# A hybrid decoder block: causal masks for two attention kinds move from TensorE matmuls to VectorE operands

## The chip, the cores and the metric

The kernel runs on one core of one Trainium2 chip. It is written in Python against the Bass and Tile libraries; a scheduler in Tile puts each engine's instructions into a fixed order when the program is built. The metric is the device time of one execution in microseconds (us), taken as the median of several runs.

Engines are named as the profile names them: PE is TensorE (PEld its weight loads), DVE is VectorE, ACT is ScalarE, POOL is GpSimd, SP is SyncE, which issues most DMAs.

## What is computed

One decoder layer on 1024 tokens of width 1024, with 16 meta tokens in front (1040 positions in all, T in the code). Three head groups work in parallel on the normalised input: stick-breaking attention (8 heads of 64), a Mamba-2 state-space mixer, and MLA (8 heads, keys of 64 + 32). Their outputs go through one output projection, and a SwiGLU feed-forward layer follows. The change touches the two attention kinds:

```python
def stick_breaking_attention(q, k, v, valid):
    ...
        mask = (kidx[None, :] < qidx[:, None]) & valid[None, :]
        z = jnp.einsum('bqhd,bkhd->bhqk', qb.astype(F32), kf) * scale
        log_1m = jnp.where(mask, jax.nn.log_sigmoid(-z), 0.0)
        between = lax.cumsum(log_1m, axis=3, reverse=True) - log_1m
        w = jnp.exp(jnp.where(mask, jax.nn.log_sigmoid(z) + between, -jnp.inf))
        return jnp.einsum('bhqk,bkhd->bqhd', w, vf)

def mla_attention(q, k, v, valid):
    ...
        mask = (kidx[None, :] <= qidx[:, None]) & valid[None, :]
        s = jnp.einsum('bqhd,bkhd->bhqk', qb.astype(F32), kf) * scale
        p = jax.nn.softmax(jnp.where(mask, s, -1e30), axis=-1)
        return jnp.einsum('bhqk,bkhd->bqhd', p, vf)
```

A query of stick-breaking attention sees the keys before itself; a query of MLA sees itself too. In a block of 128 queries only the last 128 keys need a mask; all earlier keys are visible.

## The kernel before

Numbers are kept to full precision by splitting each operand into a high part and a remainder (hi and lo, rounded fp32), so a product takes two or three matmuls. Attention is done per head in rows: a row is a block of 128 queries against all keys up to its end, 144 to 1040 columns, cut by `key_chunks` into one to three chunks of at most 512 columns, each in its own PSUM bank (`sc_ps`, a ring of three).

**Stick-breaking row** (`sb_row`, lines 688 to 705). For each chunk, from the last to the first, two matmuls give the scores (L696, L697). The chunk that ends the row gets a third one (L700): the identity times `sb_mask`, a 128 x 128 tile with -1e30 above the diagonal, which adds the mask to the last 128 columns. ScalarE then writes the sigmoid of -score/8 into the row tile `cm` (L702); a masked column becomes 1. When the row is complete, VectorE runs one scan from right to left over it (L704): `state = data0 * state + data1`, starting from 1, where data1 is a column of zeros, `zcol`, broadcast over the row. The result is the running product of the sigmoids. There are 8 heads of 8 rows, so 64 scans and 64 mask matmuls.

**MLA row** (`mla_row`, lines 983 to 1017). Three matmuls per chunk (L999 to L1001), and on the last chunk a fourth with `mla_mask` (L1004). VectorE takes the negated maximum of each chunk (L1006); if there is more than one chunk, a further small reduction takes the minimum over the chunks (L1011). That is the bias of ScalarE's exponential (L1014), which also sums each chunk; VectorE adds the sums (L1016). Again 64 rows: 24 of one chunk, 32 of two, 8 of three.

**Values.** `weighted_values` takes two rows (an odd and an even block): TensorE transposes them 128 columns at a time (L319 to L331) into the banks `ptm` and `ptg`, ScalarE and VectorE split these into hi and lo (L314, L315, L321, L322), and TensorE multiplies by the values into `pv` (L304 to L323).

**What fills the gaps.** Beside the stick-breaking rows the scheduler places dense projections (`dense_fm`, L147 to L149): the next head pair's keys and queries (L607 to L617 evacuate them), the step sizes of the state-space mixer (`step_sizes`, L428 to L461) and its convolution channels (L495 to L508). Beside MLA it places the gate units (L547 to L550). `step_sizes` transposes its result into a bank (`dtt`, L434), copies it on VectorE (`dx`, L441 to L443), and then needs exponentials on ScalarE (L445 to L447), for which ScalarE's function table is loaded and afterwards loaded back for the sigmoid.

The order on each engine comes from Tile's scheduler, which simulates a timeline from its own costs when the program is built; `high_priority` and `issue_after` push single groups. So an instruction that vanishes or changes its cost can move others on all engines.

[...]

## Time and profile before

| what | value |
|---|---|
| runs | 1745.85, 1749.13, 1754.57 us; median 1749.13 |
| profiled execution | span 1747.0 us, which is its own time here; no other is listed for it |
| mean granted TensorE clock | 0.993 of full speed |
| DMA | 222.35 MB, mean 127 GB/s |
| GpSimd busy | 719.9 us (41%) |
| stick-breaking rows | about 68 to 437 us |
| MLA rows | about 659 to 991 us |

The span runs from the first to the last instruction of one profiled execution. Busy times overlap between engines. A matmul's duration in a row reaches beyond the start of the next one, since matmuls are pipelined; how long one holds the engine is read from the distance between starts. "Releaser" is the instruction whose end let a waiting one start. In a line such as `L704 DVE TENSOR_TENSOR_SCAN cm<-cm,zcol 128x1040 ... x8 | 19.9, 2484 | 1.2` stand the source line, engine, operation, output and inputs, shape and count, then busy us in total, mean ns of one, and idle us of the engine before them.

### The profile page before, as it was taken

To read this page: it belongs to the slowest core of one execution; us is meant where nothing else is said; L and a number is where in the kernel's file an instruction comes from. 1 tells how busy PE (TensorE), PEld (TensorE's weight loads), DVE (VectorE), ACT (ScalarE), POOL (GpSimd) and SP (SyncE) were. 2 spreads that over 40 slices of the span, in tenths; PEclk is the share of its full clock that TensorE was granted. 3 is DMA by queue.
4 is the path that set the end of the run, shared out by engine and by line. 5 is a ranking of instruction groups with operands and counts; after the bars stand their busy time and mean duration, and the time that the engine had idled before them with its cause. 6 is when DMAs were issued, how large, how long until landed. Compare 5 with 4: busy or idle time off the path is not lost. (4 is left out here: it accounts for less than half of the span.)

```text
span 1747.0 us, 26605 instructions
## 1 busy us (share of the span) xinstructions
PE 1696.7 (97%) x9801; PEld 1490.7 (85%) x9801; DVE 1136.0 (65%) x1742; ACT 845.0 (48%) x1813; POOL 719.9 (41%) x514
## 2 busy tenths in 40 slices
PE   8989999999999999999999999999999999999998
PEld 7979989999987788998888888778888888878887
DVE  7777676778454654555575656975666665688644
ACT  7555565655477727666554425422222322343333
POOL 3233345344477647553321445635555455200012
PEclk9999999999999999999999999999999999999999
DMA  4222232122434556347321442123332223999602
GB/s 163 74 68 64 69 86 80 55 70 75 146 118 128 182 175 172 102 125 241 111 87 37 130 162 89 62 92 107 104 102 97 91 96 115 329 397 354 238 1 97
DMA packets 145639, 222.35 MB, mean 127 GB/s; under 512 B 24722, under 2 KB 84148, under 8 KB 145508
## 3 DMA queue, kind: packets, MB, share of 16 engines
q1 hardware_dynamic: 126112, 205.09, 36.0%
q10 hardware_dynamic: 19396, 15.56, 2.9%
q8 instruction: 77, 1.26, 0.3%
q14 instruction: 54, 0.44, 0.1%
HBM read 157.56 MB, written 63.04 MB: 126 GB/s over the span
## 5 line engine op out<-in xcount | busy, mean ns | idle before, releaser
L147 PE MATMUL d_ps<-hnh,whi 128*128 128x384 f32 (+6 forms) x744 | 249.6, 336 | 7.0 <-DVE KS L610 4.1
L148 PE MATMUL d_ps<-hnh,wlo 128*128 128x384 f32 (+6 forms) x744 | 245.5, 330 | 0.0
L149 PE MATMUL d_ps<-hnl,whi 128*128 128x384 f32 (+6 forms) x744 | 245.4, 330 | 0.0
L136 POOL TENSOR_TENSOR wlo<-wraw,whi 128x1024 fp32r<-128x1024 f32 (+1 forms) x57 | 137.1, 2405 | 231.0 <-ACT whi L134 224.4
L147 PEld LDWEIGHTS d_ps<-hnh,whi 128*128 128x128 f32 (+1 forms) x744 | 140.3, 189 | 11.9 <-issue 3.1
L148 PEld LDWEIGHTS d_ps<-hnh,wlo 128*128 128x128 f32 (+1 forms) x744 | 140.4, 189 | 2.8 <-issue 0.5
L149 PEld LDWEIGHTS d_ps<-hnl,whi 128*128 128x128 f32 (+1 forms) x744 | 140.1, 188 | 2.3
L1287 PE MATMUL b_ps<-T,wl 128*128 128x512 f32 x352 | 138.3, 393 | 1.3 <-POOL wl L1118 1.3
L1286 PE MATMUL b_ps<-T,wh 128*128 128x512 f32 x352 | 138.5, 394 | 0.8 <-ACT wh L1117 0.4
L1288 PE MATMUL b_ps<-T,wh 128*128 128x512 f32 x352 | 137.7, 393 | 1.3 <-DVE T L1118 1.3
L315 DVE TENSOR_TENSOR pl<-ptg,ph 128x512 fp32r<-128x512 f32 (+1 forms) x160 | 99.8, 627 | 41.7 <-ACT ph L314 40.5
L1117 ACT CAST op<-raw 128x1024 fp32r<-128x1024 f32 x69 | 71.3, 1050 | 111.0 <-PE d_ps L1572 73.5
L1118 DVE TENSOR_TENSOR op<-raw,op 128x1024 fp32r<-128x1024 f32 x69 | 84.2, 1230 | 43.4 <-ACT op L1117 43.4
L704 DVE TENSOR_TENSOR_SCAN cm<-cm,zcol 128x144 f32<-128x144 f32 (+3 forms) x64 | 103.5, 1622 | 8.7 <-ACT cm L702 8.4
L314 ACT CAST ph<-ptg 128x512 fp32r<-128x512 f32 (+1 forms) x160 | 85.9, 542 | 41.6 <-PE ptg L331 24.3
L1118 POOL TENSOR_TENSOR wlo<-raw,whi 128x1024 fp32r<-128x1024 f32 x18 | 46.2, 2568 | 110.0 <-ACT whi L1117 110.0
L134 ACT CAST whi<-wraw 128x1024 fp32r<-128x1024 f32 (+1 forms) x57 | 58.9, 1033 | 57.9 <-PE d_ps L149 32.3
L1118 POOL TENSOR_TENSOR wl<-raw,wh 128x512 fp32r<-128x512 f32 x46 | 75.1, 1639 | 27.3 <-ACT wh L1117 27.3
L1124 POOL TENSOR_TENSOR tt<-tt 128x512 f32<-128x512 f32 (+1 forms) x8 | 8.1, 1009 | 188.8 <-ACT tt L1642 188.7
L1117 ACT CAST wh<-raw 128x512 fp32r<-128x512 f32 x88 | 53.1, 616 | 66.1 <-PE b_ps L1288 66.0
L507 POOL TENSOR_TENSOR csig<-csig,cacc 128x384 f32<-128x384 f32 (+1 forms) x36 | 47.5, 1320 | 84.2 <-issue 40.7
L502 DVE SCALAR_TENSOR_TENSOR cacc<-d_ps,cw,cacc 128x384 f32<-128x384 f32 (+3 forms) x108 | 61.8, 572 | 29.4 <-ACT cacc L495 27.5
(442 smaller groups left out, 5176.1 us busy)
## 6 DMA issues: line engine op xcount, KB each, us to landing
raw<-in_w_down_dram SPq DMA_DIRECT2D x99, 256.0 KB, 5.4
s_hops<-gs SPq DMA_DIRECT2D x63, 256.0 KB, 2.0
raw<-s_hops SPq DMA_DIRECT2D x63, 256.0 KB, 5.4
raw<-in_w_gate_dram SPq DMA_DIRECT2D x22, 512.0 KB, 3.5
raw<-in_w_up_dram SPq DMA_DIRECT2D x22, 512.0 KB, 4.0
wraw<-in_w_o_dram SPq DMA_DIRECT2D x16, 512.0 KB, 3.6
wraw<-in_w_xbc_dram SPq DMA_DIRECT2D x12, 512.0 KB, 3.6
s_xs<-csig SPq DMA_DIRECT2D x24, 192.0 KB, 2.5
```

Of the source, the lines that this page charges most:

```text
L136: pool.tensor_tensor(lo[:, :cols], raw[:, :cols], f32(hi[:, :cols]), op=ALU.subtract)
L147: pe.matmul(ps[:m, :n], wh, mh, start=(kt == 0), stop=False)
L148: pe.matmul(ps[:m, :n], wl, mh, start=False, stop=False)
L149: pe.matmul(ps[:m, :n], wh, ml, start=False, stop=(kt == nkt - 1))
L314: act.copy(ph[:, :n], pt[:, :n])
L315: dve.tensor_tensor(pl[:, :n], pt[:, :n], f32(ph[:, :n]), op=ALU.subtract)
L704: dve.tensor_tensor_scan(rev, rev, zcol.to_broadcast([128, n_all]), 1.0, ALU.mult, ALU.add)
L1117: act.copy(hi, value)
L1118: eng.tensor_tensor(lo, value, f32(hi), op=ALU.subtract)
L1286: pe.matmul(banks[j], hi[:, ks], UH[u][k], start=start and k == 0, stop=False, skip_group_check=skip)
L1287: pe.matmul(banks[j], lo[:, ks], UH[u][k], start=False, stop=False, skip_group_check=skip)
L1288: pe.matmul(banks[j], hi[:, ks], UL[u][k], start=False, stop=stop and k == 3, skip_group_check=skip)
```

## The change

Both mask matmuls are removed. In a stick-breaking row the mask becomes the scan's second operand: `sb_mask` is now as wide as the longest row (1040 columns), zero except in the masked corner of its last 128 columns, where it is 1, and the scan computes `state = max(data0 * state, data1)`. The product never exceeds 1, so the maximum resets it to 1 at a masked column and changes nothing elsewhere. `zcol` goes.

In an MLA row the last chunk's reduction becomes `tensor_tensor_reduce`: it writes -(score + mask) back over the scores in PSUM and takes the minimum of that along the row. `mla_mask` is now 512 columns wide with -1e30 in its corner. With two chunks the reduction starts from the first chunk's result, so the small reduction over chunks remains only for rows of three. The exponential of the last chunk takes a scale of -1 to undo the negation.

The masks take some 5 KB more of each SBUF partition; the area reserved for DMA descriptors is set to 4096 bytes (last hunk).

```diff
-    sb_mask = const.tile([128, 128], F32R, name="sb_mask")
-    mla_mask = const.tile([128, 128], F32R, name="mla_mask")
-    for e, (m, base) in enumerate(((sb_mask, -1), (mla_mask, 0))):
-        full = scratch[:, 128 * (e + 1) : 128 * (e + 2)]
-        pool.memset(full, 0.0)
+    sb_mask = const.tile([128, T], F32, name="sb_mask")
+    mla_mask = const.tile([128, 512], F32, name="mla_mask")
+    for m, base, fill in ((sb_mask, -1, 1.0), (mla_mask, 0, NEG)):
+        pool.memset(m, 0.0)
+        last = m[:, m.shape[1] - 128 :]
         pool.affine_select(
-            out=full, in_=full, pattern=[[-1, 128]], compare_op=ALU.is_ge, fill=NEG,
+            out=last, in_=last, pattern=[[-1, 128]], compare_op=ALU.is_ge, fill=fill,
             base=base, channel_multiplier=1,
         )
-        act.copy(m, full)
...
-                last = c0 + n >= n_all
                 pe.matmul(ps[:, :n], qs, Kh[:, c0 : c0 + n], start=True, stop=False)
-                pe.matmul(ps[:, :n], qs, KSh[:, c0 : c0 + n], start=False, stop=not last)
-                if last:
-                    m0 = n_all - 128 - c0
-                    pe.matmul(ps[:, m0 : m0 + 128], identr, sb_mask, start=False, stop=True)
-                    n = n_all - c0
+                pe.matmul(ps[:, :n], qs, KSh[:, c0 : c0 + n], start=False, stop=True)
                 act.activation(cm[:, c0 : c0 + n], ps[:, :n], AF.Sigmoid, scale=-0.125)
             rev = cm[:, 0:n_all][:, ::-1]
-            dve.tensor_tensor_scan(rev, rev, zcol.to_broadcast([128, n_all]), 1.0, ALU.mult, ALU.add)
+            dve.tensor_tensor_scan(rev, rev, sb_mask[:, T - n_all :][:, ::-1], 1.0, ALU.mult, ALU.max)
...
-                last = c0 + n >= n_all
+                last = x == nch - 1
...
-                pe.matmul(ps[:, :n], qh, KL[:96, c0 : c0 + n], start=False, stop=not last)
+                pe.matmul(ps[:, :n], qh, KL[:96, c0 : c0 + n], start=False, stop=True)
                 if last:
-                    m0 = n_all - 128 - c0
-                    pe.matmul(ps[:, m0 : m0 + 128], identr, mla_mask, start=False, stop=True)
-                    n = n_all - c0
-                dve.tensor_reduce(sm[:, x : x + 1], ps[:, :n], AX.X, ALU.max, negate=True)
+                    dve.tensor_tensor_reduce(
+                        ps[:, :n], ps[:, :n], mla_mask[:, 512 - n :], -1.0, sm[:, 0:1] if nch == 2 else -NEG,
+                        ALU.add, ALU.min, sm[:, x : x + 1],
+                    )
+                else:
+                    dve.tensor_reduce(sm[:, x : x + 1], ps[:, :n], AX.X, ALU.max, negate=True)
                 banks.append((ps, c0, n))
-            bias = sm[:, 0:1]
-            if nch > 1:
+            bias = sm[:, nch - 1 : nch]
+            if nch > 2:
                 bias = sm[:, 3:4]
                 dve.tensor_reduce(bias, sm[:, 0:nch], AX.X, ALU.min)
             for x, (ps, c0, n) in enumerate(banks):
                 acc = total if nch == 1 else sm[:, 4 + x : 5 + x]
-                act.activation(pr[:, c0 : c0 + n], ps[:, :n], AF.Exp, bias=bias, accum_out=acc)
+                sign = -1.0 if x == nch - 1 else 1.0
+                act.activation(pr[:, c0 : c0 + n], ps[:, :n], AF.Exp, scale=sign, bias=bias, accum_out=acc)
...
-    nc = bacc.Bacc("TRN2", target_bir_lowering=False, num_devices=1)
+    nc = bacc.Bacc("TRN2", target_bir_lowering=False, num_devices=1, dynamic_dma_scratch_size=4096)
```

Line numbers of the changed kernel are 3 to 8 lower than before from the masks on. The instruction orders of the two programs differ at many places before the feed-forward part. Three of them are shown, each as the order of before and then of the change.

VectorE at the first rows of stick-breaking attention, head 0, where the copies of the step sizes stand. `cm` is a row of scores, `dx` the step sizes, `dtt` the bank that they come from, `pm` the split of the meta columns; SCALAR_TENSOR_TENSOR is how the order names the scan.

```order
L704 SCALAR_TENSOR_TENSOR cm<-cm,zcol 128x400
L441 MEMSET dx 128x16
L322 TENSOR_TENSOR pm<-ptm,pm 16x256
L704 SCALAR_TENSOR_TENSOR cm<-cm,zcol 128x528
L442 COPY dx<-dtt 16x16
L443 COPY dx<-dtt 128x128
```
```order
L696 SCALAR_TENSOR_TENSOR cm<-cm,sb_mask 128x400
L696 SCALAR_TENSOR_TENSOR cm<-cm,sb_mask 128x528
L438 MEMSET dx 128x16
L319 TENSOR_TENSOR pm<-ptm,pm 16x256
L439 COPY dx<-dtt 16x16
L440 COPY dx<-dtt 128x128
```

The scan over 528 columns stood between the meta columns' split and the copies of the step sizes; it now stands ahead of both.

TensorE at the same place, from the transposes of the meta columns (`ptm`) on. `K`, `KS` and `Q` are the split keys and queries, `d_ps<-hnh,whi` the dense projection of the next keys, which goes on behind the last row of each piece.

```order
L319 MATMUL ptm<-identr,cm 16x128
L320 MATMUL ptm<-identr,cm 16x128
L696 MATMUL sc_ps<-K,Q 128x256
L697 MATMUL sc_ps<-KS,Q 128x256
L700 MATMUL sc_ps<-sb_mask,identr 128x128
L696 MATMUL sc_ps<-K,Q 128x272
L697 MATMUL sc_ps<-KS,Q 128x272
```
```order
L316 MATMUL ptm<-identr,cm 16x128
L317 MATMUL ptm<-identr,cm 16x128
L692 MATMUL sc_ps<-K,Q 128x256
L693 MATMUL sc_ps<-KS,Q 128x256
L692 MATMUL sc_ps<-K,Q 128x400
L693 MATMUL sc_ps<-KS,Q 128x400
L692 MATMUL sc_ps<-K,Q 128x384
L693 MATMUL sc_ps<-KS,Q 128x384
```

Here the score tiles of 400 and 384 columns, which stood behind most of the dense projection, come before it; the 272-column tile that stood here has moved ahead of the transposes.

VectorE among the first rows of MLA, head 0. `sc_ps` is a chunk of scores, `sm` the small tile of a row's minima and sums, `inv` a row's total, `pl` the lower part of a split; ISA is how the order names the two instructions of `tensor_tensor_reduce`.

```order
L322 TENSOR_TENSOR pm<-ptm,pm 16x256
L1006 TENSOR_REDUCE sm<-sc_ps 128x1
L315 TENSOR_TENSOR pl<-ptg,ph 128x384
L1016 TENSOR_REDUCE inv<-sm 128x1
L1006 TENSOR_REDUCE sm<-sc_ps 128x1
L1011 TENSOR_REDUCE sm<-sm 128x1
```
```order
L319 TENSOR_TENSOR pm<-ptm,pm 16x256
L312 TENSOR_TENSOR pl<-ptg,ph 128x384
L1000 TENSOR_REDUCE sm<-sc_ps 128x1
L1011 TENSOR_REDUCE inv<-sm 128x1
L995 ISA sc_ps,sm<-sc_ps,mla_mask,sm 128x256
L995 ISA sm 128x1
```

The second chunk's reduction and the minimum over the two chunks have become the pair of L995: one instruction over the 256 columns and one of a single column behind it.

## Prediction

> **What bounds the kernel now.** I read the busy table first, then busy time by stretch, then what TensorE waited for, then single mask matmuls in the timeline.

> ```profile
> span 1747.0 us, 26605 instructions
> PE 1696.7 (97%) x9801; PEld 1490.7 (85%) x9801; DVE 1136.0 (65%) x1742; ACT 845.0 (48%) x1813; POOL 719.9 (41%) x514
> ```

> TensorE (PE) is busy for 97% of the span and VectorE (DVE) for 65%. A share over the whole run says little about two stages, so here are the stretches that hold the stick-breaking rows (68 to 437 us) and the MLA rows (660 to 991 us). Columns: stretch, its length, then busy time of PE, weight loads, DVE, ACT and POOL, then the granted clock.

> ```profile
> 68.00:180.00 112.00, 102.53 (x648) 95.48 (x647) 80.26 (x130) 58.98 (x129) 45.95 (x36) 0.97 0.26 74
> 180.00:310.00 130.00, 128.10 (x920) 123.39 (x920) 86.19 (x123) 77.09 (x182) 54.58 (x46) 1.00 0.27 76
> 310.00:437.00 127.00, 126.28 (x855) 122.42 (x855) 98.43 (x139) 73.83 (x168) 50.08 (x34) 1.00 0.21 67
> 660.00:770.00 110.00, 107.45 (x758) 104.84 (x757) 53.79 (x131) 77.22 (x200) 68.26 (x60) 1.00 0.45 129
> 770.00:880.00 110.00, 107.48 (x683) 96.92 (x682) 62.66 (x137) 63.15 (x164) 42.83 (x34) 1.00 0.52 162
> 880.00:991.00 111.00, 109.25 (x628) 94.26 (x628) 76.74 (x144) 56.55 (x134) 26.57 (x13) 1.00 0.28 84
> ```

> TensorE idles 9.5, 1.9, 0.7, 2.6, 2.5 and 1.8 us there: 19 us in 700, half of it in the first stretch. VectorE has 104 of 369 us free beside the stick-breaking rows and 138 of 331 beside MLA. The waits of TensorE (total, times, longest), the two largest of the stick-breaking stretch and the largest of MLA:

> ```profile
> PE d_ps L147 <- DVE KS L610: 4.1, 3, 1.8
> PE sc_ps L696 <- ACT cm L702: 3.9, 1, 3.9
> ...
> PE sc_ps L999 <- ACT pr L1014: 1.7, 2, 1.1
> ```

> No wait repeats row after row: transposes, values and dense projections of other heads fill TensorE while a row is scanned or exponentiated. What leaves TensorE there should leave the span, except just ahead of the few waits.

> **Removed: 128 mask matmuls.** The grouped rows give their count:

> ```profile
> L700 PE MATMUL sc_ps<-sb_mask,identr 128*128 128x128 f32 x64 | 15.2, 238 | 0.0
> L1004 PE MATMUL sc_ps<-mla_mask,identr 128*128 128x128 f32 x64 | 15.0, 235 | 0.0
> ```

> Their 235 ns is no price, since matmuls overlap; starts are. One MLA mask and one stick-breaking mask (start, duration), and the weight loads round the latter:

> ```profile
> 765.90 0.22 PE L1004 MATMUL sc_ps<-mla_mask,identr 128*128 128x128 f32 x1
> 765.96 0.34 PE L999 MATMUL sc_ps<-mhi 96*128 96x272 f32 x1
> 766.14 0.28 PE L1000 MATMUL sc_ps<-mhi,mlo 96*128 96x272 f32 x1
> 766.26 0.29 PE L1001 MATMUL sc_ps<-mlo,mhi 96*128 96x272 f32 x1
> ```
> ```profile
> 86.22 0.22 PE L700 MATMUL sc_ps<-sb_mask,identr 128*128 128x128 f32 x1
> 86.28 0.39 PE L147 MATMUL d_ps<-hnh,whi 128*128 128x384 f32 x1
> 86.51 0.34 PE L148 MATMUL d_ps<-hnh,wlo 128*128 128x384 f32 x1
> 86.68 0.34 PE L149 MATMUL d_ps<-hnl,whi 128*128 128x384 f32 x1
> ```
> ```profile
> 86.22 0.19 PEld L147 LDWEIGHTS d_ps<-hnh,whi 128*128 128x128 f32 x1
> 86.33 0.19 PEld L148 LDWEIGHTS d_ps<-hnh,wlo 128*128 128x128 f32 x1
> ```

> The next matmul starts 0.06 us after a mask, but the one behind it comes late. In MLA the 272-column matmul after the mask holds TensorE for 0.18 us (765.96 to 766.14), its equal for 0.12 (766.14 to 766.26). So mask and successor take 0.24 where the successor alone takes 0.12: the mask costs 0.12. In the other spot 0.29 less 0.17 gives 0.12 again. The reason is in the weight-load rows: loads follow each other by 0.11 us at the closest, and a 0.06 us matmul cannot cover one. I take 0.115 us: 128 x 0.115 = 14.7 us, 0.84% of the span. Bounds are 0.06 (7.7 us) and 0.12 (15.4 us).

> [...]

> Not all of it shortens the span: masks shortly ahead of a wait that another engine ends only lengthen that wait. Columns here: stretch, length, busy time (count) of these matmuls.

> ```profile
> 68.00:94.00 26.00, 1.38 (x6) 1.14 (x6) 0.99 0.43 108
> ```
> ```profile
> 658.00:676.00 18.00, 1.17 (x5) 0.95 (x5) 1.00 0.59 166
> ```

> Six masks lie ahead of the 3.9 us wait (ending at 93.5), five round the first MLA rows. I give back 11 x 0.115 = 1.3 us.

> **Added on VectorE, stick-breaking.** No instruction: the scan reads a 1040-wide mask where it read a broadcast column, and takes a maximum where it added. Its rows:

> ```profile
> L704 DVE TENSOR_TENSOR_SCAN cm<-cm,zcol 128x1040 f32<-128x1040 f32 x8 | 19.9, 2484 | 1.2 <-ACT cm L702 1.2
> L704 DVE TENSOR_TENSOR_SCAN cm<-cm,zcol 128x784 f32<-128x784 f32 x8 | 19.1, 2390 | 0.8 <-ACT cm L702 0.7
> L704 DVE TENSOR_TENSOR_SCAN cm<-cm,zcol 128x912 f32<-128x912 f32 x8 | 17.9, 2242 | 1.2 <-ACT cm L702 1.2
> ...
> L704 DVE TENSOR_TENSOR_SCAN cm<-cm,zcol 128x272 f32<-128x272 f32 x8 | 5.7, 716 | 0.0
> ```

> From 272 to 1040 columns it takes (2484 - 716) / 768 = 2.3 ns a column, twice the pace of the reductions below (1.0 ns). A pace so far under that of plain reading is more likely set by the running product than by the second operand, so I take no change. A third more or less is the bound; the price above is a rival below.

> **Added on VectorE, MLA.** Each of 64 rows trades a reduction of its last chunk for a fused instruction, and the order shows a second, 128x1 one behind each: "one instruction" is two. In the 32 rows of two chunks the minimum of two columns goes. Nearest rows:

> ```profile
> L1006 DVE TENSOR_REDUCE sm<-sc_ps 128x1 f32<-128x400 f32 x32 | 18.1, 565 | 5.3 <-PE sc_ps L1001 4.1 <-PE sc_ps L1004 0.8
> ...
> L1006 DVE TENSOR_REDUCE sm<-sc_ps 128x1 f32<-128x272 f32 x24 | 10.4, 434 | 3.5 <-PE sc_ps L1001 2.6 <-PE sc_ps L1004 0.7
> ...
> L1011 DVE TENSOR_REDUCE sm<-sm 128x1 f32<-128x2 f32 x32 | 4.7, 145 | 0.3
> ```
> ```profile
> L1014 ACT ACTIVATION_READ_ACCUMULATOR pr<-sc_ps,sm 128x1 f32 x112 | 22.4, 200 | 0.0
> ```

> The reduction's pace is (565 - 434) / 128 = 1.0 ns a column. The fused one makes a single pass too, so I take that pace; the far bound is the scan's 2.3. Over the last chunks' 8 x (144 + 272 + 400 + 256 + 256 + 384 + 512 + 384) = 20,864 columns that is 0 to 27 us. The second instruction lies between 0.145 us (a tiny reduction) and 0.200 (ScalarE's accumulator read): 64 of them are 9.3 to 12.8 us, less 32 x 0.145 = 4.6. VectorE gains 5 us, at the far end 35, against 138 free. In a two-chunk row the path from matmul to Exp keeps its length; in the other 32 it grows by 0.15 to 0.2 us, covered by other heads' matmuls. If a tenth of that cover fails, 1 us shows; I take 1, and 7 (a doubling of the MLA waits) as the far end.

> The rest has one answer. The sign in Exp's scale is free, and the smaller descriptor area touches nothing in the profile. The start loses two short ScalarE casts and gains wider memsets on GpSimd, which stands idle for 4.2 us ahead of its first product; that idle time hides them, and without it they would cost their own length of some 1 us.

> ```profile
> 7.80 1.28 POOL L231 TENSOR_TENSOR wk<-raw,wk 128x512 fp32r<-128x512 f32 x1 [4.16 <-ACT wk L230]
> ```

> **Moved: the order.** The scheduler laid out TensorE's order anew up to the first row sums of the feed-forward part; from there on it is unchanged.

> ```profile
> 1056.77 0.72 PE L158 MATMUL d_ps<-ones,sq 128*128 128x1 f32 x6
> ```

> At the 3.9 us wait two things move, both shown with the change: the 528-column scan now stands ahead of the step-size copies, and two score tiles are pulled forward. The rows of before:

> ```profile
> 84.84 2.73 DVE L704 TENSOR_TENSOR_SCAN cm<-cm,zcol 128x528 f32<-128x528 f32 x1
> 87.50 0.14 DVE L442 COPY dx<-dtt 16x16 f32<-16x16 f32 x1
> ```
> ```profile
> 93.54 0.70 PE L696 MATMUL sc_ps<-K,Q 128*128 128x400 f32 x1 [3.90 <-ACT cm L702]
> ...
> 95.23 0.52 PE L149 MATMUL d_ps<-hnl,whi 128*128 128x384 f32 x1
> 95.55 0.52 PE L147 MATMUL d_ps<-hnh,whi 128*128 128x384 f32 x1
> ```

> The copies end up to 2.7 us sooner, and ScalarE's table load and the sigmoid that frees the score bank hang on them. TensorE reaches its wait sooner too, having done the pulled-forward tiles. I take 1.0 us off; the bounds are 2.7 off and 1 on.

> **Sum.** -14.7 + 1.3 + 0 + 1.0 - 1.0 = -13.4 us, from 1747.0 to 1733.6. The profiled span lies 2.1 us under the median of the runs (1749.1), and I carry that over: **1736 us**, 0.77% faster. The nearest rows leave it between -7.7 + 1.3 + 7 + 1 (2 slower) and -15.4 - 2.7 (18 faster). An order that also loses a quarter of the 19 us of waits would reach 1727.

> **Rivals.** A measurement of this kernel can tell about 0.5% from no change: under 1740.4 is faster, over 1757.9 slower.

> *A mask costs only its own 0.06 us.* It frees 7.7 us, and after the other terms the run takes 1743: within 0.5%. For it speaks the step of 0.06 to the next start, against it the late matmul behind. [...]

> *The new order brings new stalls.* A stall like that of 93.5 costs more than its 3.9 us: afterwards 384-column matmuls start 0.32 us apart (95.23 to 95.55) against 0.17 before it (86.51 to 86.68). Nine to ten of them, up to 96.8, add 1.4 us. Two new stalls of 5.3 us give 1736 + 10.6 = 1747, no difference. For it speaks that the first stretch alone, with 9.5 us of idle, is reshuffled; against it that 180 to 437 us hold only 2.6 us of idle.

> *The scan pays for a true second operand.* If its 2.3 ns a column became half as much again, 8 x (144 + 272 + ... + 1040) = 37,888 columns would cost VectorE 43.6 us between 68 and 437. Its load there would go from 265 to 308 of some 362 us, and each row's transposes would wait up to 1.2 us longer. It decides from 22 us exposed, half of it: 60% gives 1736 + 26 = 1762, slower. Against it speaks the argument on the pace. For it speaks that something stretches scans already: 784 columns take longer in the mean than 912 (2390 and 2242 ns). [...]

> **Chances.** Forecast 0.68. The cheap mask 0.10 and new stalls 0.12, both within 0.5%. The scan, or anything of its size, 0.10, slower. The range of 1727 to 1750 takes in the first three cases and leaves out the last and the tails.

> **What would show it.** After: 9673 matmuls; masked chunks whose successor no longer holds 0.18 us; stick-breaking and MLA stretches shorter by about 7 us each with the same filler; scans at 2484 and 716 ns; fused instructions near 434 and 565 ns at 272 and 400 columns with 0.15 to 0.2 us behind. It is wrong if TensorE's idle time grows by over 5 us before 1057 us, if scans are over 10% longer, or if the stretch behind 1057 us changes.

## The result and the profile after

The changed kernel takes 1745.41 us (median of 20 runs, 1742.63 to 1750.33). The kernel before, on the same chip, takes 1750.86 (median of 20 runs). The ratio is 0.9969, 95% interval 0.9960 to 0.9978: 5.4 us faster, where 13.4 were forecast. The direction was right, and 1745.4 lies in the range, but 8.0 us of the forecast did not arrive.

The head of the page after:

```profile
span 1742.3 us, 26429 instructions
...
PE 1688.7 (97%) x9673; PEld 1479.6 (85%) x9673; DVE 1140.2 (65%) x1773; ACT 846.0 (49%) x1811; POOL 717.3 (41%) x514
```

There are 9673 matmuls, 128 fewer than before. VectorE has 4 us more work. The same six stretches as in the prediction (stretch, length, busy time of PE, weight loads, DVE, ACT and POOL, granted clock):

```profile
68.00:180.00 112.00, 100.68 (x609) 93.04 (x610) 79.06 (x127) 56.55 (x122) 39.56 (x34) 0.94 0.26 70
180.00:310.00 130.00, 127.69 (x915) 122.86 (x916) 89.82 (x128) 78.09 (x186) 53.94 (x45) 1.00 0.28 79
310.00:437.00 127.00, 127.00 (x858) 123.34 (x857) 95.69 (x141) 77.29 (x176) 51.00 (x37) 1.00 0.23 69
660.00:770.00 110.00, 107.42 (x758) 105.17 (x758) 58.30 (x154) 83.06 (x215) 71.49 (x63) 1.00 0.46 131
770.00:880.00 110.00, 107.04 (x664) 95.09 (x664) 65.50 (x152) 62.18 (x158) 35.95 (x29) 1.00 0.49 156
880.00:991.00 111.00, 109.86 (x619) 94.01 (x618) 74.01 (x149) 54.09 (x128) 38.40 (x16) 1.00 0.34 93
```

The five later stretches look as they did. The first one holds 609 matmuls, was 648, at a clock of 0.94, was 0.97, with 11.3 us idle, was 9.5. The waits of TensorE say where (total, times, longest):

```profile
PE sc_ps L692 <- ACT cm L694: 6.9, 2, 6.0
...
PE d_ps L144 <- DVE KS L607: 5.4, 3, 2.7
PE d_ps L1382 <- DVE hT L1091: 2.8, 1, 2.8
```

Of the 3.9 us wait ending at 93.5 us, 0.8 us is left (ending at 97.8), and a 6.0 us wait has come, almost at the start of the stick-breaking rows:

```profile
65.40 0.23 PE L692 MATMUL sc_ps<-K,Q 128*128 128x144 f32 x1
...
65.87 0.34 PE L692 MATMUL sc_ps<-K,Q 128*128 128x400 f32 x1
66.06 0.35 PE L693 MATMUL sc_ps<-KS,Q 128*128 128x400 f32 x1
72.44 0.58 PE L692 MATMUL sc_ps<-K,Q 128*128 128x256 f32 x1 [6.03 <-ACT cm L694]
72.82 0.42 PE L693 MATMUL sc_ps<-KS,Q 128*128 128x256 f32 x1
```

Three score tiles fill the three `sc_ps` banks, and nothing else can start. In before, the step-size projection stood there; its two possible banks (`d_ps`) are held by the third chunk's keys and queries until VectorE has subtracted them. VectorE at this place, before and then after:

```profile
62.88 0.55 DVE L617 TENSOR_TENSOR Q<-d_ps,Q 64x384 fp32r<-64x384 f32 x1
63.47 0.56 DVE L609 TENSOR_TENSOR K<-d_ps,K 64x384 fp32r<-64x384 f32 x1
64.04 0.56 DVE L610 TENSOR_TENSOR KS<-d_ps,K 64x384 fp32r<-64x384 f32 x1
64.63 5.31 DVE L276 TENSOR_TENSOR hnl<-xT,hnh 128x384 fp32r<-128x384 f32 x8
69.97 0.56 DVE L617 TENSOR_TENSOR Q<-d_ps,Q 64x384 fp32r<-64x384 f32 x1
```
```profile
64.53 0.55 DVE L614 TENSOR_TENSOR Q<-d_ps,Q 64x384 fp32r<-64x384 f32 x1
65.12 5.61 DVE L273 TENSOR_TENSOR hnl<-xT,hnh 128x384 fp32r<-128x384 f32 x8
70.75 0.56 DVE L606 TENSOR_TENSOR K<-d_ps,K 64x384 fp32r<-64x384 f32 x1
71.33 0.56 DVE L607 TENSOR_TENSOR KS<-d_ps,K 64x384 fp32r<-64x384 f32 x1
71.92 0.56 DVE L614 TENSOR_TENSOR Q<-d_ps,Q 64x384 fp32r<-64x384 f32 x1
```

Before, the second head's K and KS are done at 64.6 us, ahead of the eight `hnl` subtractions, so one bank is free, and projection and scores cover TensorE until the sigmoids start (it is busy for all of 60 to 76 us). After, they stand behind these eight, both banks are held until 71.9, and the sigmoids too wait for the last `hnl`. No mask matmul takes part in this: it is the order of the first phase.

### The profile page after: what moved, and what is told of

It is laid out like the page before. It is cut to its first block, busy times and chain, and to the rows that moved or that the text cites. A ratio compares the mean times of both kernels' runs of the same rounds, so it can differ in the third digit from the quotient of the medians.

```text
span 1742.3 us, 26429 instructions
## 1 busy us (share of the span) xinstructions
PE 1688.7 (97%) x9673; PEld 1479.6 (85%) x9673; DVE 1140.2 (65%) x1773; ACT 846.0 (49%) x1811; POOL 717.3 (41%) x514
## 4 chain that ended last, share of the span: by engine, by line
PE 80%; DVE 6%; DMA 6%; ACT 3%; issue 2%; POOL 2%; SPq 0%; ACTq 0%; DVEq 0%; POOLq 0%
PE d_ps L144 9%; PE d_ps L146 9%; PE d_ps L145 9%; PE b_ps L1283 8%; PE b_ps L1282 8%; PE b_ps L1281 8%; PE b_ps L1566 2%; PE b_ps L1567 2%; PE b_ps L1565 2%; PE ptg L326 2%; PE ptg L328 1%; PE pv L305 1%; PE pv L304 1%; DMA raw<-s_osbl 1%; PE sc_ps L991 1%
## 5 line engine op out<-in xcount | busy, mean ns | idle before, releaser
L696 DVE TENSOR_TENSOR_SCAN cm<-cm,sb_mask 128x144 f32<-128x144 f32 (+3 forms) x64 | 97.1, 1523 | 7.4 <-ACT cm L694 6.8
L1119 POOL TENSOR_TENSOR tt<-tt 128x512 f32<-128x512 f32 (+1 forms) x8 | 8.1, 1015 | 188.4 <-ACT tt L1637 188.2
L1282 PEld LDWEIGHTS b_ps<-T,wl 128*128 128x128 f32 x352 | 66.8, 190 | 17.4 <-POOL wl L1113 1.6
L1116 DVE TENSOR_TENSOR raw<-raw 128x512 f32<-128x512 f32 x58 | 53.2, 925 | 43.3 <-DMA raw<-in_w_gate_dram 38.4
```

The costliest lines, as they stand in the source:

```text
L696: dve.tensor_tensor_scan(rev, rev, sb_mask[:, T - n_all :][:, ::-1], 1.0, ALU.mult, ALU.max)
L1282: pe.matmul(banks[j], lo[:, ks], UH[u][k], start=False, stop=False, skip_group_check=skip)
```

## The experiments

**Theory A**: a removed mask is worth its 0.115 us, and stalls of the new order took most of the gain back. **Theory B**: a mask is worth its own 0.06 us (7.7 in all) and the order costs little. Later runs bear out A's price of a mask; where the gain went is only in part where A puts it. Each ratio is to the kernel before on the same chip.

**Last hunk alone** (`num_devices=1, dynamic_dma_scratch_size=4096`):

> The kernel before with the last hunk alone (descriptor area of 4096 bytes); every engine's order stays as it was. All theories: no change, within 1.5 us of the kernel before. It is run for what the 20 runs of before don't list: the granted clock of each run. Theory A (the removed masks were worth about 14.5 us, and new stalls with half-clock windows behind them took some 9 back): mean clock about 0.002 to 0.003 above the 0.990 of the changed kernel. Theory B (a mask was worth only 0.06 us, 7.7 in all, and the order cost little): mean clock like that of the changed kernel, 0.990.

Measured: 1.0010 (0.9999 to 1.0020), no change. The mean clock of 35 runs of before beside it is 0.9915, that of the changed kernel's 20 runs 0.9902, lower by half of what A expected. But the mean of the kernel before is 0.9907 and 0.9911 in the 11 and 17 runs beside later experiments on two other chips, so these means do not tell the two kernels apart. This run with the order of before also shows that a single trace misleads. TensorE loses 8.6 us to half clock in before's trace and 15.7 here (a granted clock of 0.50; 1 minus the clock, times busy time, summed over stretches of 2 us); the changed kernel's 14.0 is nothing special.

**Stick-breaking half alone** (the `sb_row` and `sb_mask` hunks; MLA as before):

> Stick-breaking half alone on the kernel before (mask as the scan's operand; MLA untouched). TensorE's order at the first stick-breaking rows is the one with five score tiles ahead of the step-size projection. Theory A: the 6 us wait near 66 us comes back, 64 x 0.115 = 7.4 us saved, about 3 us more idle time and 2.5 us more half clock given back up to 477 us: 2 us faster than before (0 to 4). Theory B: 64 x 0.06 = 3.8 us faster, with idle time and half clock as in before. Scans at 2484 and 716 ns at 1040 and 272 columns by both.

Measured: 1.0010 (0.9997 to 1.0022). Not 2 us faster but no change, so neither theory's number; the wait that A expected is there, 6.2 us.

**MLA half alone** (the `mla_row` and `mla_mask` hunks; stick-breaking rows as before):

> MLA half alone on the kernel before (stick-breaking rows with their mask matmuls; TensorE's first 3991 instructions stand as in before). Theory A: 64 x 0.115 = 7.4 us saved between 659 and 1057 us; the wait near 1012 us (2.8 us) and a half-clock window behind it come back and cost some 4: 3 us faster than before (1 to 5.5). Theory B: 3.8 us faster, and the stretch from 659 to 1057 us shorter by 3.8 apart from its idle time.

Measured: 0.9974 (0.9961 to 0.9987), 4.6 us faster by the ratio, with the 2.8 us wait for `hT`. By these two runs, the whole net gain of the change comes with the MLA half.

**Step-size projection put first.** In the changed kernel, the first four rows wait for that projection's matmuls:

```diff
+                        with ExitStack() as early:
+                            if p == 0 and h == 0 and i < 4:
+                                early.enter_context(tc.issue_after(dt_done[0 if i < 3 else 2]))
+                            rows.append(sb_row(Q[h], K[h], KS[h], i))
```

> The changed kernel with the step-size projection put ahead of the first score tiles; TensorE's order differs from the changed kernel in rows 369 to 551 only. Theory A (new stalls are what ate the gain): the 6.0 us wait at 66.4 us and its half-clock windows (2.5 us) go, some of the wait comes back at the later step-size chain: 4 to 8 us faster than the changed kernel, 1738 to 1741, about 0.6% under before. Theory B (masks were cheap, order counts little): within 1.5 us of the changed kernel's 1745.4.

Measured: 1.0009 (0.9995 to 1.0022): slower than the changed kernel, whose ratio is 0.9969. Both theories missed. The wait did not go; it changed its name:

```profile
65.26 0.28 PE L579 MATMUL v_ps<-wv,hnh 128*128 128x256 f32 x1
71.79 0.51 PE L144 MATMUL d_ps<-hnh,whi 128*96 128x272 f32 x1 [6.25 <-DVE KS L608]
```

Now the projection itself waits, for KS on VectorE. The first reading, "the scores stand in front of the projection", was wrong: the banks are what is missing, and VectorE's order keeps them. Beside it, a wait for KS has grown to 4.6 us (ending at 112.1; 2.7 in the changed kernel). In the traces the orders of before and of the changed kernel part on TensorE at 28.6 us, long ahead of any mask matmul, so something at the very start must have moved them. Laid side by side, the two programs differ there in nothing but the constants.

**One memset moved.** The kernel before with a single edit:

```diff
-    dve.memset(zcol, 0.0)
+    pool.memset(zcol, 0.0)
```

> The kernel before with one edit: the memset of the 128x1 column of zeros is issued on GpSimd instead of VectorE. All masks stay. By the scheduler's order this alone puts five score tiles ahead of the step-size projection, as in the changed kernel, and K, KS and Q of the third chunk behind eight hnl subtractions on VectorE; from TensorE's row 553 on its order is that of before. Theory A (the start's order, set by the constants, is what ate the stick-breaking half): a wait of about 6 us near 70 us, 3 to 8 us slower than before. Theory B (the order costs nothing, the stick-breaking masks were simply worth little): within 1.5 us of before.

Measured: 1.0036 (1.0022 to 1.0049), 6.3 us slower. Every mask is still on TensorE, and the new order with its wait is there all the same:

```profile
65.40 5.69 DVE L276 TENSOR_TENSOR hnl<-xT,hnh 128x384 fp32r<-128x384 f32 x8
71.12 0.56 DVE L609 TENSOR_TENSOR K<-d_ps,K 64x384 fp32r<-64x384 f32 x1
```
```profile
66.74 0.22 PE L700 MATMUL sc_ps<-sb_mask,identr 128*128 128x128 f32 x1
72.81 0.58 PE L696 MATMUL sc_ps<-K,Q 128*128 128x256 f32 x1 [5.85 <-ACT cm L702]
```

Up to the first mask matmul TensorE's order is that of the changed kernel. A 128x1 memset (0.06 us on VectorE in before's trace) is not worth 6 us of work, so the price is that of the order. The memset is one entry in the timeline that the scheduler simulates; how the simulation gets from there to this order is not shown. In the changed kernel other constants changed too; that the missing memset alone moves its start was not run.

**The changed kernel with the start of before.** The constants of before are still made, though no longer used, and the wide masks are built behind the first projections:

```diff
+    dve.memset(zcol, 0.0)
+    stand = const.tile([128, 256], F32R, name="stand")
+    ...  (two 128x128 masks filled and cast into stand, as before)
...
     p0_st.close()
+    for m, base, fill in ((sb_mask, -1, 1.0), (mla_mask, 0, NEG)):
+        ...
```

> The changed kernel with the start of before: the column of zeros and the two cast 128x128 masks are still made (and not used), the wide masks are built behind the first projections. TensorE's first 396 instructions are those of before. Theory A: no 6 us wait near 66 us; 6 us (the MLA half as measured) and 64 x 0.115 = 7.4 us less 1 us for masks ahead of the 3.9 us wait: 1735 to 1739, about 0.7% under before. Theory B: no faster than the MLA half alone, 1743, or only by 64 x 0.06 = 3.8 at most (1740 to 1743).

Measured: 0.9921 (0.9907 to 0.9935), median 1737.54: 13.8 us faster than before by the ratio, and faster than the changed kernel, whose interval starts at 0.9960. VectorE is back in the order of before, K and KS ahead of `hnl`:

```profile
63.91 0.56 DVE L610 TENSOR_TENSOR K<-d_ps,K 64x384 fp32r<-64x384 f32 x1
64.49 0.56 DVE L611 TENSOR_TENSOR KS<-d_ps,K 64x384 fp32r<-64x384 f32 x1
65.08 5.43 DVE L277 TENSOR_TENSOR hnl<-xT,hnh 128x384 fp32r<-128x384 f32 x8
```

The 6.0 us wait is gone, and before's wait of 3.9 us is back (3.7, ending at 93.2). That 13.8 comes close to the prediction's 13.4 is in part luck. The first MLA row and the first row sums of the feed-forward part, in the changed kernel and then in this run:

```profile
656.12 0.69 PE L991 MATMUL sc_ps<-mhi 96*128 96x144 f32 x3 [1.16 <-ACT mhi L971]
1049.35 0.72 PE L155 MATMUL d_ps<-ones,sq 128*128 128x1 f32 x6
```
```profile
658.88 1.14 PE L1003 MATMUL sc_ps<-mhi 96*128 96x144 f32 x3 [2.09 <-ACT mhi L983]
1051.09 0.72 PE L159 MATMUL d_ps<-ones,sq 128*128 128x1 f32 x6
```

Up to the row sums this run is hardly ahead of the changed kernel: 1051.1 us against 1049.4, or 1040.7 against 1041.9 with the loss to half clock taken off. TensorE's idle time up to there is 40.2 us against 40.7. The lead arises behind them, where no mask stood: 685.1 us to the end, against 692.9 in the changed kernel and 690.3 in before. The table below comes back to this.

**The same, and the `hT` wait at 1015 us taken away** (the two products of `rraw` with `grow` behind the last addition to `hT`):

```diff
+        added = last_on(DVE)
...
+            with tc.issue_after(added):
                 eng.tensor_tensor(x, x, inv[:, s], op=ALU.mult)
```

> As the kernel with the start of before, and the two products of rraw with grow on VectorE are held behind the last hT addition of the output projection, where the changed kernel runs them ahead of two such additions (TensorE waits 2.75 us at 1015 us for one). Theory A: that wait goes, the products' result is then later by 1 to 2 us and the feed-forward start waits for a part of it: 0 to 3 us faster than the kernel with the start of before. Theory B: the wait reappears in full at the last output rows, no change.

Measured: 0.9916 (0.9901 to 0.9931), not told apart from the run above. The wait at 1015 us is gone (idle time between the last MLA score and the feed-forward row sums falls from 2.8 to 0.2 us), and a wait for `hT` near 819 us grew from 1.4 to 2.4:

```profile
PE d_ps L148 <- DVE hT L1103: 2.4, 1, 2.4
```

Whether the 2.8 us are worth anything stays open.

**Stick-breaking half with the start of before**, which closes a table of two edits:

> Stick-breaking half alone (MLA with its mask matmuls) with the start of before: column of zeros and cast 128x128 masks still made, the wide mask built behind the first projections. Closes the table of stick-breaking half by start. Theory A (the removed masks are worth 0.115 us each and the start's order is a separate price): 64 x 0.115 = 7.4 us less about 1 for masks ahead of waits, 1743 to 1745, 6 to 7 us under before. Theory B (the stick-breaking half and the start's order do not simply add): within 3 us of before.

Measured: 0.9964 (0.9947 to 0.9981).

| ratio to before | start of before | new start |
|---|---|---|
| masks on TensorE | 1 | 1.0036 |
| stick-breaking half | 0.9964 | 1.0010 |

The half brings 0.36% (6.3 us), the start takes 0.36% (6.3 us), and together they leave 0.1%, within their intervals of the sum. (The two new starts are not quite the same order: TensorE's differ at a few places from 29 us on.) It looks as if the start had eaten the stick-breaking gain, but the traces do not put the times there. Each row below is one trace; the last column is the mean distance of starts of the feed-forward part's 512-column matmuls, some 2700 of them, at full clock and with no wait between:

| trace | first MLA row, us | row sums to the end, us | 512-column step, ns |
|---|---|---|---|
| before | 659.4 | 690.3 | 230.8 |
| last hunk | 657.4 | 691.8 | 230.6 |
| MLA half | 657.0 | 691.4 | 230.8 |
| one memset moved | 664.8 | 690.8 | 230.7 |
| changed kernel | 656.1 | 692.9 | 231.1 |
| stick-breaking half | 655.6 | 695.0 | 231.4 |
| projection first | 662.3 | 692.8 | 231.5 |
| start of before | 658.9 | 685.1 | 229.5 |
| the same, `hT` wait away | 654.5 | 687.2 | 229.4 |
| stick-breaking half, start of before | 655.6 | 688.5 | 229.4 |

The middle columns include half clock, which varies by some us from trace to trace. With the stick-breaking masks on TensorE, the new start costs 5 to 8 us by the first MLA row. With these masks gone it costs little there: 656.1 and 655.6 us with the new start, 658.9, 654.5 and 655.6 with the old one, and idle time up to there is 30.0 and 30.1 us against 28.1 to 29.0. The 6.0 us wait mostly stands in place of the 3.9 us one.

The lead of the last three kernels over the changed kernel and the stick-breaking half comes mostly from the feed-forward part, which no edit was meant to touch. Its matmuls step 1.3 ns closer there than in before, which is some 3.5 us over 2700 of them; in the changed kernel they step 0.4 ns wider, some 1 us. The steps fall into three groups by the constants that the kernels hold: those of before (with MLA's mask widened or not), those without the column of zeros, and the old ones together with the wide stick-breaking mask. Where the constants leave the other tiles in memory may be the cause; no run tested it. So the sum in the table of ratios is in part a coincidence.

**The price of a mask by itself.** The kernel before with 308 more matmuls in the feed-forward products, of 128 and of 32 columns (`C`):

```diff
+                if k in (0, 2):
+                    pe.matmul(banks[j][:, :C], identr, zeros, start=False, stop=False, ...)
```

> The kernel before with 308 more mask-like matmuls (identity times 128 columns of zeros) in the feed-forward gate and up products, each followed by a 512-column matmul; nothing is left out. Theory A (a mask costs its successor's weight load, 0.115 us): 308 x 0.115 = 35 us slower. Theory B (only its own 128 columns, 0.06 us): 308 x 0.06 = 18 us slower.

> As the kernel with 308 additional 128-column matmuls in the feed-forward products, but with 32 columns each. Theory A (the price is the wait for the successor's weight load): about the same as with 128 columns, 29 to 35 us slower than before. Theory B (the price follows the columns): a quarter of it, 8 to 9 us slower.

Measured: 1.0181 (1.0158 to 1.0204) with 128 columns, 31.7 us, 0.103 each; 1.0170 (1.0142 to 1.0199) with 32, 29.8 us, 0.097 each. A quarter of the columns costs nearly the same. One of each, with the 512-column matmul behind it and the start of the next:

```profile
1231.18 0.22 PE L1290 MATMUL b_ps<-zeros,identr 128*128 128x128 f32 x1
1231.24 0.45 PE L1291 MATMUL b_ps<-T,wl 128*128 128x512 f32 x1
1231.53 0.39 PE L1292 MATMUL b_ps<-T,wh 128*128 128x512 f32 x1
```
```profile
1230.35 0.18 PE L1290 MATMUL b_ps<-zeros,identr 128*128 128x32 f32 x1
1230.38 0.47 PE L1291 MATMUL b_ps<-T,wl 128*128 128x512 f32 x1
1230.69 0.39 PE L1292 MATMUL b_ps<-T,wh 128*128 128x512 f32 x1
```

The short one steps 0.06 or 0.03 us, and its successor then holds 0.29 or 0.31 where its equals hold 0.23: 0.35 or 0.34 together, less 0.23, is 0.12 or 0.11. In before's trace the weight load of a mask's successor is followed by the next load after a median of 0.109 us (stick-breaking) and 0.110 us (MLA), as in the prediction's rows (86.22 to 86.33); the totals of 0.097 and 0.103 us lie near that, not near the short matmul's own step.

## Why the prediction was wrong, step by step

- **128 masks at 0.115 us: right.** Over all masks of before with no wait among their two successors (63 and 61 of 64), the same subtraction gives a median of 0.11 in both kinds; only ahead of another 128-column matmul (14 of them) is it less, 0.06 to 0.08. The extra matmuls give 0.103. In the traces, TensorE's time up to the row sums, without idle time and loss to half clock, falls from 1016.0 and 1015.0 us (before, last hunk) to 1001.2, by 14.3. The cheap-mask rival falls. After the change, the successor's late step is gone: a 272-column matmul behind the last product of a row holds 0.13, the next one 0.13.

```profile
757.16 0.40 PE L993 MATMUL sc_ps<-mlo,mhi 96*128 96x512 f32 x1
757.39 0.29 PE L991 MATMUL sc_ps<-mhi 96*128 96x272 f32 x1
757.52 0.29 PE L992 MATMUL sc_ps<-mhi,mlo 96*128 96x272 f32 x1
757.65 0.29 PE L993 MATMUL sc_ps<-mlo,mhi 96*128 96x272 f32 x1
```

- **The scan at no price: right.** All 64 take 97.1 us, before 103.5; 2394 ns at 1040 columns, was 2484, though 782 at 272, was 716. Its rival falls. The fused instruction costs what its neighbours did (453 and 584 ns at 272 and 400 columns, was 434 and 565), and its second part 132 ns, less than the 145 to 200 taken:

```profile
L696 DVE TENSOR_TENSOR_SCAN cm<-cm,sb_mask 128x1040 f32<-128x1040 f32 x8 | 19.1, 2394 | 1.4 <-ACT cm L694 1.3
...
L995 DVE DVE_READ_ACCUMULATOR2_ANT sm<- 128x1 f32 x64 | 8.4, 132 | 0.2
...
L995 DVE CUSTOM_DVE_ANT_0 sc_ps<-sc_ps,mla_mask 128x400 f32<-128x400 f32 x8 | 4.7, 584 | 0.2 <-PE sc_ps L993 0.2
...
L995 DVE CUSTOM_DVE_ANT_0 sc_ps<-sc_ps,mla_mask 128x272 f32<-128x272 f32 x8 | 3.6, 453 | 0.7 <-PE sc_ps L993 0.7
```

- **1.0 us exposed beside MLA: not seen.** Idle time over the MLA rows is 7.9 us, was 8.2. The 1.3 us given back by masks ahead of waits was not measured by itself.
- **"The rest has one answer", and the order at -1.0 us: the steps that failed.** The prediction priced the start's lost constants as work, at nothing, named two ScalarE casts and left out the column's memset on VectorE. It looked at the order only at the 3.9 us wait, took that wait's shortening, and bounded the term at 1 us slower. In place of that 1.0 us off, TensorE's idle time ahead of the row sums grew to 40.7 us, from 36.0 and 33.6 in the two traces with before's order: 4.7 to 7.1 us more. The first of the new waits sits over 20 us ahead of the place that was examined. The moved memset alone, with every mask in place, costs 6.3 us (2.2 to 4.9 thousandths). How much of the changed kernel's waits is the start's stays open: with the old start they are hardly less, 40.2 us. What would have told of the first wait was at hand: VectorE's order between 57 and 73 us, and the question who frees the two `d_ps` banks.
- **The rival that came true** is "the new order brings new stalls", given 0.12. Its price, two stalls of 5.3 us, gave 1747, 1.6 us from the result. The two are there: 6.0 us at 72.4, and 2.75 at 1015. That the price fits so well is in part chance, since the first of them mostly replaces the 3.9 us wait and the feed-forward part added 1.9 us of its own. Its argument against, that 180 to 437 us hold little idle time, spoke of the wrong stretch. The sign that the prediction named, idle time ahead of 1057 us grown by over 5 us, was nearly met against before's trace and met against that of the last hunk: 36.0 and 33.6 us, then 40.7, summed over the gaps between TensorE's records.
- **Nothing changes behind 1057 us: right for the order, not for the time.** From there to the end the profiled execution takes 2.7 us longer than before's, with TensorE in the same order. Half clock costs 6.4 us there, 3.8 in before, but 6.7 in the run of the last hunk alone, which has before's order: it varies from one execution to the next. The 512-column steps, 231.1 ns against 230.8 and 230.6, are a second part, about 1 us, and recur in the other kernels without the column of zeros.
- **The account.** Against the mean of the two traces with before's order (before and last hunk alone), the changed kernel takes 7.9 us less up to the row sums: 14.3 less matmul time, 5.9 more idle time, 0.5 more half clock. Behind them it takes 1.9 us more: 2.4 more matmul time, 1.0 more half clock, 1.6 less idle time. That makes 6.0 faster, 5.4 measured. The forecast had 13.4 less and nothing. The forecast had the stick-breaking and the MLA stretch each about 7 us shorter: against the same two traces the time from the first MLA row to the row sums is 4.2 and 7.1 us shorter, the time up to the first MLA row only 3.2 and 1.3.

## What to carry to other kernels

Where a scheduler orders the program, an instruction that goes is also an entry less in its simulation: compare the order of every engine from the first line that differs, not only where work was removed, and for each moved group ask which banks it frees and who needs them. To measure an edit, time order and edit apart, and compare stretch by stretch, with those that no edit should touch: here one moved memset cost 6.3 us, nearly the 7.4 that 64 mask matmuls are worth, but a table of ratios alone put a gain of the feed-forward part down to the start. A short matmul among 512-column ones costs, in these runs, 0.103 us with 128 columns and 0.097 with 32: close to the 0.11 us between two weight loads, and hardly a matter of its columns.

## What had not been expected of the hardware

```profile
1062.00:1064.00 2.00, 2.00 (x8) 1.58 (x7) 0.00 (x0) 0.00 (x0) 2.00 (x2) 0.69 0.00 0
1064.00:1066.00 2.00, 2.00 (x8) 1.61 (x7) 0.22 (x1) 0.00 (x0) 0.55 (x1) 0.50 0.62 180
```

It follows the one-column row sums (1056.8 to 1061.4 us); whether these bring it on, no run tested, and in the changed kernel's trace no such block follows them (the next starts at 1074.1). The lost shares there (0.62, 1.0 and 0.08 us) add up to 1.7, half of 3.4. How much half clock takes varies between executions (8.6 and 15.7 us in the two traces with before's order): 0.996 to 0.987 of full clock and 1744 to 1756 us in 35 runs of before, and there a thousandth of mean clock goes with 1.3 us (a straight line through them). In the traces of before and of the changed kernel every block but the final one takes 3.413 or 6.827 us, and the starts lie whole multiples of 3.4133 us apart.
